# An encoder step on one core: the first weight unit ordered by hand, the seven-product scheme from the third group on, and a reciprocal root moved from GpSimd to VectorE

## The chip, the cores and the metric

The program runs on one core of a Trainium2 chip. The metric is the device time of one execution in microseconds; the time given is a median over runs, and the profile is of one further execution.

## The reference, cut to what matters

Two layers are applied to 512 prompt tokens and 64 sample tokens of width 1024, all in float32:

```python
# layer A (forgetting attention), layer B (gated MLP), each as x + mixer(rmsnorm(x)) @ w_out
z = h @ w_in_a            # q, k, v, gate (4 x 1024 columns) and 8 columns of forget logits
q, k = rmsnorm(q), rmsnorm(k)                     # per head of 128
logf = log_sigmoid(z[..., 4096:] + b_f)           # cumulated to a bias of the scores
o = softmax(q k^T * scale + f_q - f_k, causal) v  # sample rows also see 1024 cached keys
x = x + (o * silu(gate)) @ w_out_a

z = h @ w_in_b            # u, v, gate (3 x 2048 columns), v in 8 groups of 256 columns
v = rmsnorm(v)                                    # per group and row: needs 1/sqrt(mean square)
mixed = ws[g] (128 x 128, masked) applied to v over the rows of a chunk, + bs[g]
x = x + (u * mixed * silu(gate)) @ w_out_b
```

## The kernel before, in words

**Products.** Every float32 operand is split into a high part (rounded on ScalarE, `split`, L124) and a low part (the rest, on VectorE, L125). Each product is three TensorE matmuls: high by high, high by low, low by high. Weights come in units of 1 MB (two buffers `wraw`), and are split in pieces of 128x512 into `whi` and `wlo`; up to 8 pieces are held ahead (`PIECES`). Layer A has 20 units: four times k, q and v of two heads, four of the gate, four of the output. Layer B has 24 units (for each of 8 groups v, gate and u) and 8 of the output.

**Order.** Nothing is ordered by the program's text alone: when the kernel is built, a planner simulates the engines with its own costs and puts every instruction into its engine's queue at the moment when, in its simulation, it is ready; text order and a raised priority decide between ready ones. On the chip each queue then runs in exactly that order, and the head of a queue that waits holds up all behind it. Text order follows a clock of matmul time (`self.clock`): `later(delay, fn)` puts a step's text behind as much matmul work, with raised priority, except for the patient ones. `manual_schedule` makes the text order of an engine's instructions binding, and a manual dependency without a semaphore (`NOSYNC`) binds the order of two of them.

**First unit (k of heads 0 and 1).** The weights arrive in four DMAs, the tokens in tiles of 128 rows (the second tile's DMA between the second and third weight DMA, L208 to L211). A token tile is transposed in eight TensorE instructions (`turn_x`), scaled, and split. Tile 0 and the four weight pieces are ordered by hand in `run`; the turns of tiles 1 to 4 are called from `project_qk` through `next_x` with raised priority, and the planner places them. Squares of the tokens (`token_squares`, ScalarE, 1.06 us each) have no tie. The forget logits, carried in 16 extra columns, are finished in `forget`.

**MLP group (`group_in`).** `rows_product` makes v for four tiles of 128 rows (24 matmuls each) and the sample tile (16). The squares' sums go to `vz`; GpSimd scales them (L1175), VectorE makes the first guess of the root and GpSimd does three Newton rounds of four instructions (`rsqrt_pool`, L156 to L159). Then `split_scaled` makes `bvhi` (ScalarE) and `bvlo` (VectorE), and `mix` (raised priority, `MIX_DELAY` later) multiplies them by the group's 128x128 matrix into `s`, which VectorE takes to `mixed`. The gate unit is evicted through Silu into `gr`; GpSimd multiplies `gr` by `mixed` (L1215, 128x576, twice a group); the u unit is evicted by a product with `gr` into `pr` (L1201). Two of the four `mm` buffers in PSUM hold v until `split_scaled` has read it.

Gate and u of group 0 are plain: two halves of 128 columns by two halves of 288 tokens, 8 x 3 matmuls each, 96 in all (`cols_product`). From group `FAST_GROUP` = 1 on a seven-product scheme does it in 7 x 12 = 84 (`fast_product`), which needs sums of the weights (L236 to L241, VectorE) and of the tokens (`token_sums`: ten VectorE steps of 128x1152 in the still unused part of `pr`, L393, and four splits to `tparts`, in steps of `SUMS` = 2.4 us of the clock from group 0's gate on, as patient steps).

**Output of layer B (`out_b`).** It reuses the memory of the tokens and of `tparts` for the rows `xf`, the results `y` (3 buffers) and the split products `prhi`, `prlo`; a tile waits for what lay in its place.

Of the kernel before, what the change touches and what calls it, by code (L numbers as in the profile page):

```python
# [12 lines left out]
F32 = mybir.dt.float32  # L13
# [10 lines left out]
KT = 8  # L24
# [17 lines left out]
FORGET = (7.2, 11.7)  # L42
MIX_DELAY = 6.0
TURN = (5.3, 0.7)
# [4 lines left out]
PIECES = 8  # L49
FAST_GROUP = 1  # L50
SUMS = 2.4
# [8 lines left out]
class Program:  # L60
    def __init__(self, tc, io):
        self.tc = tc
        self.nc = tc.nc
        self.io = io
        self.clock = 0.0
        self.tasks = []
        self.count = 0
        self.count_y = 0
        self.patient = (self.sample_cache_values, self.gates_out, self.token_step)
# [52 lines left out]
    def split(self, hi, lo, src):  # L122

        self.nc.scalar.copy(hi, src)  # L124
        self.nc.vector.tensor_tensor(lo, src, hi.bitcast(F32), op=ALU.subtract)  # L125
# [7 lines left out]
    def rsqrt(self, z, pool, tag):  # L133

        v = self.nc.vector
        shape = list(z.shape)
        y = pool.tile(shape, F32, name=tag + "_y", tag=tag + "_y")
        t = pool.tile(shape, F32, name=tag + "_t", tag=tag + "_t")
        v.tensor_scalar(y.bitcast(I32), z.bitcast(I32), 1, None, op0=ALU.logical_shift_right)
        v.tensor_scalar(y.bitcast(I32), y.bitcast(I32), -1, MAGIC, op0=ALU.mult, op1=ALU.add)  # L140
        for _ in range(3):
            v.tensor_tensor(t, y, y, op=ALU.mult)
            v.scalar_tensor_tensor(t, in0=t, scalar=-0.5, in1=z, op0=ALU.mult, op1=ALU.mult)
            v.scalar_tensor_tensor(y, in0=t, scalar=1.5, in1=y, op0=ALU.add, op1=ALU.mult)
        return y

    def rsqrt_pool(self, z, pool, tag):

        v, p = self.nc.vector, self.nc.gpsimd
        shape = list(z.shape)  # L150
        y = pool.tile(shape, F32, name=tag + "_y", tag=tag + "_y")
        t = pool.tile(shape, F32, name=tag + "_t", tag=tag + "_t")
        v.tensor_scalar(y.bitcast(I32), z.bitcast(I32), 1, None, op0=ALU.logical_shift_right)
        v.tensor_scalar(y.bitcast(I32), y.bitcast(I32), -1, MAGIC, op0=ALU.mult, op1=ALU.add)
        for _ in range(3):
            p.tensor_tensor(t, y, y, op=ALU.mult)  # L156
            p.tensor_tensor(t, t, z, op=ALU.mult)  # L157
            p.tensor_scalar(t, t, -0.5, 1.5, op0=ALU.mult, op1=ALU.add)  # L158
            p.tensor_tensor(y, y, t, op=ALU.mult)  # L159
        return y  # L160
# [106 lines left out]
    def weights(self):  # L267

        self.held = 0
        self.fill()  # L270
# [16 lines left out]

    def rows_product(self, out, xhi, xlo, tile_no, w, extra=None):

# [5 lines left out]
        nkt = len(whi)  # L295
        for kt in range(nkt):
            s = slice(128 * tile_no, 128 * (tile_no + 1))
# [81 lines left out]
    def token_sums(self):  # L379
# [95 lines left out]
    def turn_x(self, pool, i):  # L475

        for half in range(2):
            self.turn_x_half(pool, i, half)

    def turn_x_half(self, pool, i, half):  # L480
# [51 lines left out]
    def forget(self, pool):  # L532
# [121 lines left out]
    def project_qk(self, p, is_q):  # L654
        nc, io, pool = self.nc, self.io, self.proj
        w = self.weights()
        name = "q" if is_q else "k"
# [29 lines left out]
        for grp in range(2):  # L687
            if first:
                src = pool.tile([128, 512], F32, name="nrm", tag="nrm", bufs=2)
                for i in range(2):  # L690
                    self.next_x()
                    ps = self.ps_mm()[:, :272]
                    self.rows_product(ps, *self.xparts, 2 * grp + i, w, self.whi0)
                    nc.scalar.copy(src[:, 256 * i:256 * (i + 1)], ps[:, :256])
                    self.forget_columns(2 * grp + i, ps)
            else:
                src = self.ps_mm()
                for i in range(2):
                    self.next_x()
                    self.rows_product(src[:, 256 * i:256 * (i + 1)], *self.xparts, 2 * grp + i, w)  # L700
# [4 lines left out]
        if first:  # L705
            self.rows_product(ps[:, :272], *self.xparts, 4, w, self.whi0)
            self.sample_rows(ps, pool, raw)
# [9 lines left out]
        for grp in range(3):  # L717
# [5 lines left out]
            for j in range(k):  # L723
                c = slice(128 * j, 128 * (j + 1))
                nc.vector.scalar_tensor_tensor(nrm[:, c], in0=srcs[grp][:, c], scalar=r[:n, 4 * grp + j:4 * grp + j + 1],
                                               in1=gain[:n], op0=ALU.mult, op1=ALU.mult)
            if not is_q and grp < 2:
# [11 lines left out]

    def next_x(self):  # L740
        if self.x_steps:
            self.x_steps.pop(0)()

# [368 lines left out]
    def group_in(self, g):  # L1112
# [49 lines left out]
        for grp in range(3):  # L1162
# [7 lines left out]
            else:  # L1170
# [25 lines left out]
        def gate(m, half, src):  # L1196
            nc.scalar.activation(grs[m][:, HALF * half:HALF * (half + 1)], src, AF.Silu)

        def product(m, half, src):
            out = self.pr[:, 2 * g + m, HALF * half:HALF * (half + 1)]  # L1200
            nc.vector.tensor_tensor(out, src, grs[m][:, HALF * half:HALF * (half + 1)], op=ALU.mult)  # L1201

# [26 lines left out]
    def out_b(self, pool):  # L1229
# [3 lines left out]
        for i in range(5):  # L1233
            n = 128 if i < 4 else NS
            xs.append(pool.tile([128, D], F32, name=f"xf{i}")[:n])
            nc.sync.dma_start(xs[i], self.x1d[i, :n, :])
        ys = pool.tile([128, 3, 512], F32, name="y")
        lows = pool.tile([NS, 512], F32, name="lows")

        parts = {}  # L1240
        for k in [14, 15, None] + list(range(14)):
            if k is None:
                pool.tile([128, 256], F32, name="unused")
                continue
            parts[k] = (pool.tile([128, NT + NS], F32R, name=f"prhi{k}"), pool.tile([128, NP], F32R, name=f"prlo{k}"))
# [9 lines left out]
        for j in range(2):  # L1255
            c = slice(512 * j, 512 * (j + 1))

            def finish(i, ps):
                y = ys[:xs[i].shape[0], self.count_y % 3, :]
                self.count_y += 1  # L1260
# [7 lines left out]
    def run(self):  # L1268
# [5 lines left out]
        with ExitStack() as top:  # L1274
# [47 lines left out]

            def step(i):
                with tc.high_priority(offset=XPRI):
                    self.turn_x(xp, i + 1)
                if i == 3:
                    for j in range(5):
                        self.token_squares(xp, j)
                    self.r_a, self.rb_a = self.token_scales(self.ss, "a")

            self.x_steps = [lambda i=i: step(i) for i in range(4)]
            self.project_qk(0, False)
# [81 lines left out]
```

## Time and profile before

| what | value |
|---|---|
| runs shown | median 823.99 us (822.27, 823.99, 825.94) |
| the profiled execution | 820.57 us |
| its span, first to last instruction | 818.6 us |
| TensorE busy | 786.3 us, 96% |
| VectorE, ScalarE, GpSimd busy | 67%, 46%, 24% |
| mean granted TensorE clock | 0.987 |

Times in the rows are microseconds from the span's start. A busy share says little of the kernel as a whole: TensorE is busy nearly always, so what can be saved there is idle time, time at the lower clock, or matmuls. In brackets behind an instruction stands how long its engine was idle before it and what ended the wait.

### The profile page before, as it was taken

The page shows a single profiled execution, that of the slowest core. Times are in us where ns is not written, and L with a number is a line of the kernel's source. Part 1 is how long each engine was busy: PE and PEld are TensorE (multiplying, and loading weights), DVE is VectorE, ACT ScalarE, POOL GpSimd, SP SyncE. Part 2 cuts the span into 40 slices and gives each one's busy share as a digit, 9 for nine tenths or more (in the row PEclk, how much of TensorE's full clock was granted, in tenths as well). Part 3 has the DMA queues.
Part 4 walks back from the last instruction along what each step waited for, and adds up shares of the span by engine and source line. Part 5 has one row for each costly group of instructions (what it writes and reads, how often), then busy time and mean ns, then how long its engine had stood idle before and what let it go on. Part 6 is the DMA issues. An engine that isn't in the chain of part 4 may idle for free.

```text
span 818.6 us, 14697 instructions
## 1 busy us (share of the span) xinstructions
PE 786.3 (96%) x5542; PEld 743.0 (91%) x5542; DVE 551.0 (67%) x1335; ACT 373.0 (46%) x875; POOL 195.4 (24%) x342
## 2 busy tenths in 40 slices
PE   6999999999999999998977999999999999899998
PEld 5999999999999998887967999999999999788886
DVE  4787767867675778449786677687778686862312
ACT  4545546464564557334441627363544445631210
POOL 1100723213235564000232323232232423100000
PEclk8999999999999999999989999999999999999999
DMA  8898653546434652644030233132333131533201
GB/s 214 110 111 146 179 90 85 116 95 61 100 67 144 205 169 80 216 149 170 7 116 8 67 100 113 56 110 65 103 104 111 56 106 55 187 136 117 95 1 58
DMA packets 73814, 87.60 MB, mean 107 GB/s; under 512 B 5224, under 2 KB 62336, under 8 KB 73744
## 3 DMA queue, kind: packets, MB, share of 16 engines
q1 hardware_dynamic: 73744, 86.67, 40.7%
q8 instruction: 43, 0.70, 0.3%
q14 instruction: 27, 0.22, 0.1%
HBM read 76.63 MB, written 10.03 MB: 106 GB/s over the span
## 4 chain that ended last, share of the span: by engine, by line
PE 85%; DVE 5%; POOL 3%; issue 2%; DMA 2%; ACT 2%; SPq 1%; POOLq 0%; DVEq 0%; ACTq 0%
PE mm L78 65%; PE s L78 13%; PE tr L82 4%; PE tr L78 2%; DMA wraw<-w_in_a 1%; DVE wlo L125 1%; DMA ts<-negs 1%; PE mm L82 1%; ACT whi L124 1%; POOL v_y L159 1%; POOL v_t L156 1%; DVE gt L982 1%; POOL v_t L157 1%; POOL v_t L158 0%; ACT sqv L1221 0%
## 5 line engine op out<-in xcount | busy, mean ns | idle before, releaser
L125 DVE TENSOR_TENSOR wlo<-wraw,whi 128x512 fp32r<-128x512 f32 x236 | 161.1, 702 | 91.1 <-ACT whi L124 87.5
L124 ACT CAST whi<-wraw 128x512 fp32r<-128x512 f32 x236 | 140.5, 620 | 158.3 <-PE mm L78 92.8
L78 PE MATMUL mm<-whi,xhi 128*128 128x256 f32 (+1 forms) x728 | 205.5, 287 | 4.1 <-DVE pr L1201 2.6
L78 PE MATMUL mm<-wlo,xhi 128*128 128x256 f32 x728 | 204.0, 285 | 0.0
L78 PE MATMUL mm<-whi,xlo 128*128 128x256 f32 (+1 forms) x640 | 183.2, 287 | 0.0
L78 PEld LDWEIGHTS mm<-whi,xhi 128*128 128x128 f32 x728 | 138.9, 191 | 5.4 <-DVE pr L1201 2.8
L78 PEld LDWEIGHTS mm<-wlo,xhi 128*128 128x128 f32 x728 | 138.7, 191 | 0.5
L78 PEld LDWEIGHTS mm<-whi,xlo 128*128 128x128 f32 x640 | 121.7, 190 | 0.6
L78 PE MATMUL mm<-xhi,whi 128*128 128x288 f32 x360 | 110.3, 307 | 0.8 <-DVE fq L371 0.8
L78 PE MATMUL mm<-xlo,whi 128*128 128x288 f32 x360 | 107.3, 298 | 0.0
L78 PE MATMUL mm<-xhi,wlo 128*128 128x288 f32 x360 | 107.2, 298 | 0.0
L78 PEld LDWEIGHTS mm<-xhi,whi 128*128 128x128 f32 x360 | 68.7, 191 | 1.4 <-DVE fq L371 1.1
L78 PEld LDWEIGHTS mm<-xlo,whi 128*128 128x128 f32 x360 | 68.8, 191 | 0.1
L78 PEld LDWEIGHTS mm<-xhi,wlo 128*128 128x128 f32 x360 | 68.6, 191 | 0.1
L770 POOL TENSOR_SCALAR tt<-nf,fq 128x128 f32<-128x128 f32 (+3 forms) x32 | 39.2, 1230 | 119.7 <-PE tr L82 66.6
L78 PE MATMUL mm<-thi,whi 128*128 128x288 f32 x224 | 67.0, 299 | 0.0
L78 PE MATMUL mm<-thi,wlo 128*128 128x288 f32 x224 | 66.3, 296 | 0.0
L78 PE MATMUL mm<-tlo,whi 128*128 128x288 f32 x224 | 66.2, 295 | 0.0
L1215 POOL TENSOR_TENSOR gr<-gr,mixed 128x576 f32<-128x576 f32 x16 | 27.4, 1720 | 93.4 <-DVE mixed L1156 93.1
L78 PE MATMUL mm<-whi,prhi 128*128 128x512 f32 x112 | 44.0, 393 | 1.8 <-ACT prhi L1251 1.2
L78 PE MATMUL mm<-wlo,prhi 128*128 128x512 f32 x112 | 43.8, 391 | 0.0
L78 PEld LDWEIGHTS mm<-tlo,whi 128*128 128x128 f32 x224 | 42.1, 188 | 0.0
(317 smaller groups left out, 1631.8 us busy)
## 6 DMA issues: line engine op xcount, KB each, us to landing
wraw<-w_in_b SPq DMA_DIRECT2D x24, 1024.0 KB, 5.2
wraw<-w_in_a SPq DMA_DIRECT2D x15, 1024.0 KB, 9.7
wraw<-w_out_b SPq DMA_DIRECT2D x8, 1024.0 KB, 5.2
kr<-cache_k SPq DMA_DIRECT2D x4, 1024.0 KB, 7.2
vr<-cache_v SPq DMA_DIRECT2D x4, 1024.0 KB, 5.3
wraw<-w_out_a SPq DMA_DIRECT2D x4, 1024.0 KB, 5.1
ts<-negs SPq DMA_DIRECT2D x8, 272.0 KB, 6.6
k_prompt<-nrm SPq DMA_DIRECT2D x8, 256.0 KB, 6.2
```

What stands on the lines that cost most here:

```text
L78: self.nc.tensor.matmul(out, lhs, rhs, start=start, stop=stop, skip_group_check=resumed)
L82: self.nc.tensor.transpose(out, src, self.ident[:n, :n])
L124: self.nc.scalar.copy(hi, src)
L125: self.nc.vector.tensor_tensor(lo, src, hi.bitcast(F32), op=ALU.subtract)
L156: p.tensor_tensor(t, y, y, op=ALU.mult)
L157: p.tensor_tensor(t, t, z, op=ALU.mult)
L159: p.tensor_tensor(y, y, t, op=ALU.mult)
L770: nc.gpsimd.tensor_scalar(t[:, :n], head["nf"][:, :n], self.fq[:, i, h:h + 1], None, op0=ALU.add)
L982: eng.tensor_tensor(g, g, self.ot[:, h, :], op=ALU.mult)
L1215: nc.gpsimd.tensor_tensor(grs[dt], grs[dt], mixed[dt], op=ALU.mult)
```

## The change

Constants: `MIX_DELAY` 6.0 to 3.0, `FAST_GROUP` 1 to 2. For v the GpSimd root is removed, and scaling and root run on VectorE. The first unit's TensorE order is written out (`first_rows`), its next unit's split is called behind the last token tile, with a tie; token squares are tied behind the casts of the next token tile; the forget chain behind the last norm of the first keys. The steps of the token sums are tied behind the latest eviction of a gate or u half, and use the `pr` rows of groups 4 to 7 as scratch (groups 2 to 5 before). `out_b` has four `y` buffers and no filler tile.

```diff
-MIX_DELAY = 6.0
+MIX_DELAY = 3.0
-FAST_GROUP = 1
+FAST_GROUP = 2
...
     def split_piece(self, n, i, src):
...
         self.split(hi, lo, src)
+        if n == 1:
+            self.tc.add_manual_dep(self.last_cast.ins, self.turned[4].ins.name, NOSYNC, reason="the tokens go first")
...
     def token_sums(self):
...
-        d3, d1, e3, e1 = (self.pr[:, 4 + 2 * n:6 + 2 * n, :].rearrange("p a (b t) -> p (a b) t", b=2) for n in range(4))
+        d3, d1, e3, e1 = (self.pr[:, 8 + 2 * n:10 + 2 * n, :].rearrange("p a (b t) -> p (a b) t", b=2) for n in range(4))
+        def behind(inst):
+
+            if self.last_taken is not None:
+                self.tc.add_manual_dep(inst.ins, self.last_taken.ins.name, NOSYNC, reason="spread out")
         def step(eng, out, a, b, op):
-            eng.tensor_tensor(out, a, b, op=op)
+            behind(eng.tensor_tensor(out, a, b, op=op))
         def done(n, src):
-            self.split(*self.tparts[n], src)
+            hi, lo = self.tparts[n]
+            behind(nc.scalar.copy(hi, src))
+            nc.vector.tensor_tensor(lo, src, hi.bitcast(F32), op=ALU.subtract)
...
     def token_squares(self, pool, i):
-        self.nc.scalar.activation(sq[:n], self.xin[i][:n], AF.Square, accum_out=self.ss[:n, i:i + 1])
+        square = self.nc.scalar.activation(sq[:n], self.xin[i][:n], AF.Square, accum_out=self.ss[:n, i:i + 1])
+        self.tc.add_manual_dep(square.ins, self.turned[min(i + 1, 4)].ins.name, NOSYNC, reason="the casts go first")
...
     def forget(self, pool):
-        nc.vector.tensor_tensor(f, self.fx, self.r_a.unsqueeze(2).broadcast_to(shape), op=ALU.mult)
+        first = nc.vector.tensor_tensor(f, self.fx, self.r_a.unsqueeze(2).broadcast_to(shape), op=ALU.mult)
+        self.tc.add_manual_dep(first.ins, self.last_norm.ins.name, NOSYNC, reason="the keys go first")
...
+    def first_rows(self, i, w):
+
+        a, b, c = range(0, 4), range(4, 6), range(6, 8)
+        order = {0: ((0, a), 1, (0, b), (1, a), (0, c)), 1: (2, (1, b), (1, c)), 2: ((2, a), 3, (2, b), (2, c)),
+                 3: ((3, a), 4, (3, b), (3, c))}[i]
+        with self.tc.manual_schedule(engines={mybir.EngineType.PE}):
+            for step in order:
+                if isinstance(step, int):
+                    self.turn_x(self.xpool, step)
+                else:
+                    n, kts = step
+                    if n not in self.first_sums:
+                        self.first_sums[n] = self.ps_mm()[:, :272]
+                    self.rows_product(self.first_sums[n], *self.xparts, n, w, self.whi0, kts)
+        if i == 3:
+            for j in range(5):
+                self.token_squares(self.xpool, j)
+            self.r_a, self.rb_a = self.token_scales(self.ss, "a")
+            self.fill()
+        return self.first_sums.pop(i)
...
     def group_in(self, g):
-        nc.gpsimd.tensor_scalar(z, z, 1.0 / 256, EPS, op0=ALU.mult, op1=ALU.add)
-        y = self.rsqrt_pool(z, small, "v")
+        nc.vector.tensor_scalar(z, z, 1.0 / 256, EPS, op0=ALU.mult, op1=ALU.add)
+        y = self.rsqrt(z, small, "v")
...
     def out_b(self, pool):
-        ys = pool.tile([128, 3, 512], F32, name="y")
+        ys = pool.tile([128, 4, 512], F32, name="y")
-        for k in [14, 15, None] + list(range(14)):
-            if k is None:
-                pool.tile([128, 256], F32, name="unused")
-                continue
+        for k in [14, 15] + list(range(14)):
```

## Rows read from the trace of the kernel before

**Rows 1.** Stretches: us; busy of PE, PEld, DVE, ACT, POOL; clock, DMA share, GB/s.
```profile
10.00:20.00 10.00, 6.36 (x33) 5.74 (x34) 6.49 (x13) 6.64 (x12) 0.00 (x0) 0.66 1.03 255
410.00:420.00 10.00, 8.78 (x67) 8.55 (x65) 9.20 (x14) 4.82 (x9) 2.78 (x6) 1.00 0.62 204
420.00:440.00 20.00, 13.53 (x75) 13.02 (x76) 14.26 (x28) 5.71 (x11) 5.41 (x18) 0.74 0.07 21
440.00:450.00 10.00, 7.41 (x62) 7.21 (x62) 5.71 (x8) 0.58 (x2) 2.77 (x2) 1.00 0.02 5
480.00:520.00 40.00, 40.00 (x318) 39.88 (x317) 30.91 (x62) 19.05 (x46) 10.52 (x23) 1.00 0.27 86
705.00:710.00 5.00, 3.49 (x26) 3.12 (x24) 3.91 (x11) 2.05 (x4) 1.55 (x2) 1.00 0.66 210
710.00:715.00 5.00, 3.61 (x13) 2.38 (x14) 5.00 (x10) 5.00 (x10) 1.71 (x1) 1.00 0.61 230
```

**Rows 2.** Timeline of TensorE, group 0: start, duration, instruction, idle before and releaser.
```profile
423.28 0.80 PE L78 MATMUL s<-wst,bvhi 128*128 128x256 f32 x2 [4.50 <-ACT bvhi L1225]
426.68 0.69 PE L78 MATMUL s<-wst,bvlo 128*128 128x128 f32 x2 [1.49 <-DVE bvlo L1226]
439.03 0.35 PE L78 MATMUL s<-whi,xhi 128*128 128x256 f32 x1 [1.70 <-DVE mixed L1156]
443.75 0.39 PE L78 MATMUL mm<-whi,xhi 128*128 128x256 f32 x1 [2.59 <-DVE pr L1201]
```

**Rows 3.** Chain that ended last, group 0: start, duration, what ran or was waited for.
```profile
406.90 8.47 PE mm L78 x64
...
415.56 1.81 DMA wsr<-ws
...
427.37 6.16 PE mm L78 x28
```

**Rows 4.** Timelines of GpSimd and VectorE in group 0, around the root and the gate product.
```profile
412.94 0.51 POOL L1175 TENSOR_SCALAR vz<-vz 128x5 f32<-128x5 f32 x1 [7.52 <-ACT sqv L1221]
...
414.58 1.35 DVE L393 TENSOR_TENSOR pr<-pr,xhi 128x1152 f32<-128x1152 f32 x1
...
439.29 3.48 POOL L1215 TENSOR_TENSOR gr<-gr,mixed 128x576 f32<-128x576 f32 x2
439.60 1.92 DVE L238 TENSOR_TENSOR wraw<-wraw 128x512 f32<-128x512 f32 x1
```

**Rows 5.** Timelines of GpSimd and TensorE in group 5.
```profile
610.52 0.54 POOL L1175 TENSOR_SCALAR vz<-vz 128x5 f32<-128x5 f32 x1 [9.51 <-ACT sqv L1221]
...
616.44 0.20 POOL L159 TENSOR_TENSOR v_y<-v_y,v_t 128x5 f32<-128x5 f32 x1
...
617.20 0.50 PE L78 MATMUL s<-wst,bvhi 128*128 128x256 f32 x2 [0.17 <-ACT bvhi L1225]
```

**Rows 6.** Timeline of VectorE: first and last of eleven root instructions, twice.
```profile
54.65 0.17 DVE L139 TENSOR_SCALAR h_y<-hz 128x10 int32<-128x10 int32 x1
...
57.59 0.17 DVE L144 SCALAR_TENSOR_TENSOR h_y<-h_t,h_y 128x10 f32<-128x10 f32 x1
...
87.08 0.17 DVE L139 TENSOR_SCALAR h_y<-hz 128x10 int32<-128x10 int32 x1
...
92.11 0.16 DVE L144 SCALAR_TENSOR_TENSOR h_y<-h_t,h_y 128x10 f32<-128x10 f32 x1
```

**Rows 7.** Timelines of TensorE and ScalarE, first unit.
```profile
16.45 1.09 PE L82 MATMUL tr<-ident,xt 128*128 128x128 f32 x4 [2.10 <-DVE wlo L125]
...
11.46 1.06 ACT L506 ACTIVATE xsq<-xt 128x1024 f32<-128x1024 f32 x1 [2.46 <-DMA xt<-x_prompt]
...
14.47 0.62 ACT L124 CAST whi<-wraw 128x512 fp32r<-128x512 f32 x1 [0.31 <-DMA wraw<-w_in_a]
...
24.36 1.14 ACT L124 CAST whi<-wraw 128x512 fp32r<-128x512 f32 x2 [0.60 <-DMA wraw<-w_in_a]
```

**Rows 8.** Timeline of GpSimd, end of group 7.
```profile
708.45 3.26 POOL L1215 TENSOR_TENSOR gr<-gr,mixed 128x576 f32<-128x576 f32 x2 [14.02 <-DVE mixed L1156]
```

More of the change, by code (lines that the diff above doesn't have):

```diff
@@ L67, in __init__ @@
         self.count = 0
+        self.last_taken = None
         self.count_y = 0
@@ L122, in split @@
     def split(self, hi, lo, src):
-        self.nc.scalar.copy(hi, src)
+        self.last_cast = self.nc.scalar.copy(hi, src)
         self.nc.vector.tensor_tensor(lo, src, hi.bitcast(F32), op=ALU.subtract)
@@ L144, in rsqrt @@
             v.scalar_tensor_tensor(y, in0=t, scalar=1.5, in1=y, op0=ALU.add, op1=ALU.mult)
[L145 to L159, printed above, removed]
         return y
@@ L264, in split_piece, with weights @@
         self.split(hi, lo, src)
+        if n == 1:
+            self.tc.add_manual_dep(self.last_cast.ins, self.turned[4].ins.name, NOSYNC, reason="the tokens go first")
         self.queue.append(([hi[:, q, :] for q in range(k)], [lo[:, q, :] for q in range(k)]))
-    def weights(self):
+    def weights(self, fill=True):
         self.held = 0
-        self.fill()
+        if fill:
+            self.fill()
         his, los = [], []
@@ L284, in block, with rows_product @@
         return self.queue.pop(0)
-    def rows_product(self, out, xhi, xlo, tile_no, w, extra=None):
+    def rows_product(self, out, xhi, xlo, tile_no, w, extra=None, kts=range(KT)):
         whi, wlo = w
@@ L295, in rows_product @@
         nkt = len(whi)
-        for kt in range(nkt):
+        for kt in kts:
             s = slice(128 * tile_no, 128 * (tile_no + 1))
@@ L478, in turn_x @@
             self.turn_x_half(pool, i, half)
+        self.turned[i] = self.last_cast
     def turn_x_half(self, pool, i, half):
@@ L655, in project_qk @@
         nc, io, pool = self.nc, self.io, self.proj
-        w = self.weights()
+        w = self.weights(p or is_q)
         name = "q" if is_q else "k"
@@ L690, in project_qk @@
                 for i in range(2):
-                    self.next_x()
-                    ps = self.ps_mm()[:, :272]
-                    self.rows_product(ps, *self.xparts, 2 * grp + i, w, self.whi0)
+                    ps = self.first_rows(2 * grp + i, w)
                     nc.scalar.copy(src[:, 256 * i:256 * (i + 1)], ps[:, :256])
@@ L698, in project_qk @@
                 for i in range(2):
-                    self.next_x()
                     self.rows_product(src[:, 256 * i:256 * (i + 1)], *self.xparts, 2 * grp + i, w)
@@ L705, in project_qk @@
         if first:
-            self.rows_product(ps[:, :272], *self.xparts, 4, w, self.whi0)
+            with self.tc.manual_schedule(engines={mybir.EngineType.PE}):
+                self.rows_product(ps[:, :272], *self.xparts, 4, w, self.whi0)
             self.sample_rows(ps, pool, raw)
@@ L724, in project_qk @@
                 c = slice(128 * j, 128 * (j + 1))
-                nc.vector.scalar_tensor_tensor(nrm[:, c], in0=srcs[grp][:, c], scalar=r[:n, 4 * grp + j:4 * grp + j + 1],
-                                               in1=gain[:n], op0=ALU.mult, op1=ALU.mult)
+                self.last_norm = nc.vector.scalar_tensor_tensor(
+                    nrm[:, c], in0=srcs[grp][:, c], scalar=r[:n, 4 * grp + j:4 * grp + j + 1], in1=gain[:n],
+                    op0=ALU.mult, op1=ALU.mult)
             if not is_q and grp < 2:
@@ L738, in forget_columns @@
         self.nc.vector.tensor_reduce(self.fx[:n, i, :], cols, axis=AX.X, op=ALU.add)
-    def next_x(self):
-        if self.x_steps:
-            self.x_steps.pop(0)()
+    def first_rows(self, i, w):
+        a, b, c = range(0, 4), range(4, 6), range(6, 8)
+        order = {0: ((0, a), 1, (0, b), (1, a), (0, c)), 1: (2, (1, b), (1, c)), 2: ((2, a), 3, (2, b), (2, c)),
+                 3: ((3, a), 4, (3, b), (3, c))}[i]
+        with self.tc.manual_schedule(engines={mybir.EngineType.PE}):
+            for step in order:
[10 more added lines that the diff above has]
+            self.r_a, self.rb_a = self.token_scales(self.ss, "a")
+            self.fill()
+        return self.first_sums.pop(i)
     def begin_attention(self, p):
@@ L1196, in gate @@
         def gate(m, half, src):
-            nc.scalar.activation(grs[m][:, HALF * half:HALF * (half + 1)], src, AF.Silu)
+            self.last_taken = nc.scalar.activation(grs[m][:, HALF * half:HALF * (half + 1)], src, AF.Silu)
         def product(m, half, src):
             out = self.pr[:, 2 * g + m, HALF * half:HALF * (half + 1)]
-            nc.vector.tensor_tensor(out, src, grs[m][:, HALF * half:HALF * (half + 1)], op=ALU.mult)
+            self.last_taken = nc.vector.tensor_tensor(out, src, grs[m][:, HALF * half:HALF * (half + 1)], op=ALU.mult)
         def form(take):
@@ L1258, in finish @@
             def finish(i, ps):
-                y = ys[:xs[i].shape[0], self.count_y % 3, :]
+                y = ys[:xs[i].shape[0], self.count_y % 4, :]
                 self.count_y += 1
@@ L1321, in run @@
                 self.warm_up(scratch, WARM[1])
[L1323 to L1331, printed above, removed]
+            self.xpool, self.first_sums, self.turned = xp, {}, {}
             self.project_qk(0, False)
```

## The prediction, made before the changed kernel ran

> **What bounds the kernel now.** I first read the table of stretches. From 480 to 520 us TensorE is busy 40.00 of 40 us and takes 318 instructions, 0.126 us each, while VectorE is busy 31 us and ScalarE 19 [rows 1]: in the MLP groups the matmul stream is the limit, and a faster GpSimd, VectorE or ScalarE is worth nothing there unless TensorE waits for it. So I looked for stretches in which TensorE is not full. There are three, and the change touches all of them: 10 to 20 us (33 instructions in 10 us, granted clock 0.66), 420 to 440 us (75 instructions in 20 us, clock 0.74), and 705 to 715 us (7.10 busy of 10 us) [rows 1].
>
> Then the timeline of TensorE for the worst, group 0 of the MLP: four waits, 4.50, 1.49, 1.70 and 2.59 us, the first two for `bvhi` and `bvlo`, the scaled v, the third for `mixed`, the last for a product taken out of PSUM [rows 2]. The chain that ended last says what lies behind the first: not a matmul but the DMA of `wsr`, 1.81 us [rows 3]. GpSimd's queue shows why. It scaled `vz` at 412.94, after waiting 7.52 us for the squares [rows 4]; the Newton rounds of the root stood behind a clearing of the next group's `wsr`, whose data had yet to land. VectorE was crowded as well: a token sum of 1.35 us started at 414.58, between the two instructions of the first guess [rows 4]. TensorE got its `bvhi` at 423.28, 10.3 us after `vz`.
>
> **The first MLP group (root on VectorE, sums tied, `MIX_DELAY`).** What is lost: the first wait of 4.50 us began at 418.78, so 1.2 us of it lie before 420. From 420 to 440 there are 75 instructions, which at 0.126 us take 9.4 us, so 10.6 us are lost [rows 1]; behind 440 the last wait adds 2.6 [rows 2]. Together 14.4 us. About 10.3 of these are the four waits, the rest is the clock: 28 matmuls of 288 columns took 6.16 us (0.220 each) behind the wait, 64 of them 8.47 us (0.132 each) ahead of it [rows 3].
>
> With the change the root has no GpSimd instruction, so the wait for `wsr` is no longer in the chain. The eleven VectorE root instructions exist in the trace on 128x10: 3.1 us from first to last in one place, 5.2 us in another, amid other VectorE work [rows 6]. The token sums (fourteen steps, ten of 1.35 us) go behind evictions of halves, one per 24 matmuls of 0.132 us, so at most two or three fall into the root instead of a stretch that is busy 9.20 of 10 us [rows 1]. Scale, root and two scaling steps then end some 6 us after the squares instead of 10.3, and the squares themselves start earlier, because the row sums before them no longer queue behind sums of tokens. TensorE meanwhile has the rest of the gate half to do, and the planner's placing of `mix` was only 4.5 us too early. If the scaled v comes in time, `mixed` and the gate product follow at once, and the third and fourth wait go too. What is late next is VectorE itself: the remaining sums must be done before group 2's gate, a whole group later (of 299 instructions in the seven-product form, 112 for v, 168 for gate and u, 18 for `mix`, 1 turn, 37.7 us at 0.126, and 24 matmuls more in the plain form), so they have room. I take 12.9 us, leaving 1.5 us (one sum of 1.35 us in the wrong place). Bounds: 0 (the planner again places `mix` too early) and 14.4.
>
> What it costs: group 1 is plain, 2 x 12 = 24 matmuls of 288 columns more, at 0.132 us [rows 3]: +3.2 us. It is on the path, as TensorE is full there. Against it stand six casts and six low parts fewer and eight sums of weights fewer in that group; they lie beside matmuls, and I cost them at nothing.
>
> **The later groups.** In group 5 `vz` starts at 610.52 and GpSimd's last root instruction at 616.44, and TensorE waited 0.17 us for `bvhi` [rows 5]. The planner's place for `mix` thus fits the chain almost exactly. On VectorE the chain is 1 to 3 us shorter by the two examples [rows 6], the planner sees that too, and TensorE stays full: 0 us. Eight groups get 12 small instructions each, about 0.2 us apart, some 2.4 us of a group's 37.7; VectorE has a quarter of its time free [rows 1], and nobody waits for it. If that cover is gone, it costs up to the rival below.
>
> A rule of the Trainium skill bears on this. The trace first: while GpSimd ran the two gate products (3.48 us from 439.29), a VectorE sum of 128x512 took 1.92 us, more than a token sum of 128x1152 (1.35) [rows 4]. The Trainium skill, "SBUF — State Buffer", in its section on the two sides of SBUF, says that VectorE and GpSimd share a port pair under an exclusive lock: a VectorE instruction with two SBUF inputs and a GpSimd one that reads SBUF exclude each other for a whole instruction. By that rule the root moved to VectorE, three of whose steps square a tile in SBUF, could be held by a gate product, one product at most (about 1.7 us). In group 7 the products start at 708.45 [rows 8], far from any root, so I add nothing; the rule only makes the rival below a little likelier.
>
> **The first unit.** From 10 to 20 us 33 instructions make 4.2 us of full-rate work; the second token tile is there only at 11.5, so at most 10 - 4.2 - 1.5 = 4.3 us can come back [rows 1]. Two reasons are visible. ScalarE stood 2.46 us before a token square at 11.46 with casts queued behind it, and TensorE stood 2.10 us at 16.45 before the turn of the third token tile, with products of tile 0 behind it in the queue [rows 7]. The ties put the squares behind the casts, and the hand order puts 24 products of tile 0 and 12 of tile 1 ahead of that turn. The limit that stays is the fourth weight piece, cast at 14.47 when it landed [rows 7]. I estimate 3 us from this. Against it: the next unit's weights landed and were cast at 24.36, ahead of the last token tile [rows 7]; now these casts follow the last tile's, which I put at about 27 us, and the squares may come ahead of them. TensorE reaches them at about 30, so I charge 1 us. Net -2.0 us; bounds -4.3 and +2.5 (all four casts late at 0.6 us each). The forget chain moves behind the keys' norms, some 6 us later; it lies beside the q products, where TensorE is full, and I cost it at nothing.
>
> **The end.** In group 7 the gate products start at 708.45 after waiting 14.02 us for `mixed` [rows 8], and TensorE idles 2.9 us between 705 and 715 [rows 1]. An earlier `mix` brings that forward by what the root saves, 1 to 3 us: I take -1.5, bounds 0 and -2.9. The new layout in `out_b` shifts each split product by 1 KB, so that it overlaps two of the token sums' tiles; they are read for the last time at least 24 matmuls before the end of group 7, which hides it, except for the last one.
>
> **The sum.** -12.9 + 3.2 - 2.0 - 1.5 = -13.2 us. The profiled execution took 820.57 us (span 818.6 and 2 us around it), so it would take 807.4; the median of the runs is 3.4 us above that execution, so 811 us is forecast. With all bounds at the good end (-14.4, -4.3, -2.9) it is -18.4, or 806.
>
> **Rivals.**
>
> *Half of it stays.* TensorE's place for `mix` is the planner's, and it was 4.5 us wrong in group 0. With the tied sums still falling into VectorE's queue, the wait could shrink only to half. For: VectorE is the busiest helper there [rows 1]. Against: the `wsr` wait, the part the planner missed most, is gone. -7.0 + 3.2 - 1.0 - 0.7 = -5.5: 818.5 us.
>
> *The change does not do what it says.* The wait in group 0 stays whole, because something else is as late as the root was; only 24 matmuls, the first unit and the end count: +3.2 - 2.0 - 1.5 = -0.3: 823.7 us.
>
> *The first unit drops to the lower clock.* The hand order has small waits at each weight piece. In 10 to 20 us the granted clock was 0.66, so a part ran at the lower of the two levels, 1.2 GHz, after waits of about 2 us [rows 1, 7]. With 60 matmuls more at 0.22 instead of 0.126 us (5.6 us), the first unit costs about +4 instead of -2: 817 us. Against: the waits of 1.70 and 2.59 us at 439 and 444 us [rows 2] left the clock at 1.00 from 440 to 450 [rows 1]. The Trainium skill, "TensorE: Matmul & The Clock Gate" (section on PSUM-queue depth-cycling), tells of a kernel whose clock swung between its two levels because TensorE idled briefly and often between groups of matmuls. By that rule the first unit would be slowed as in this rival; the waits just named do not bear it out.
>
> *Slower.* `MIX_DELAY` lets `mix` stand 3 us earlier in TensorE's queue, in every group, and in group 5 it had 0.17 us to spare the wrong way [rows 5]. If the real VectorE chain, in a queue that is three quarters full, is no shorter than GpSimd's was (5.2 us is close to the 5.9 between 610.52 and 616.44 [rows 5, 6]) and the planner thinks it is, TensorE waits up to 3 us in each of the seven later groups: +21 us, 832 us. It makes the kernel slower by over 0.5% from (13.2 + 4.1) / 7 = 2.5 us a group on. Against: in group 5 `mix` began 6.7 us behind the scaling of `vz`, which itself waits for the last rows of v, so it stood more than 6 us behind v: the planner goes by readiness, and the delay is only a floor.
>
> **How the numbers follow.** Forecast 0.60 (alone 804 to 816), half 0.14, first unit 0.07, no change 0.08, slower 0.11. What a measurement can tell from no change is about 0.5%, 4.1 us: forecast, half and first unit are faster, 0.81; same 0.08; slower 0.11. The range 804 to 822 takes in the first three.
>
> **What would show it.** Right: no wait for `bvhi` in group 0 and clock 1.00 from 410 to 450; more than 60 instructions of TensorE from 10 to 20 us; 24 matmuls more; a group still takes 38 us from group 2 on. Wrong: waits before `mix` in every group, or a wait for `whi` near 30 us, or VectorE's sums late for group 2.

## The result, and the profile after

The changed kernel takes 815.88 us (median; 813.93 to 817.89) against 824.59 us beside it: ratio 0.9897, interval 0.9859 to 0.9936, so 8.7 us or 1.0% faster. The forecast was 811 us, the range 804 to 822; the time lies at the edge of the band of the forecast alone (804 to 816). The profiled execution took 817.46 us (820.57 before), with a span of 815.7 us and a mean granted clock of 0.985. TensorE has 5566 matmuls in it, 24 more than before, GpSimd 157 us of work instead of 195.

The sum hides two opposite movements. I used two instructions that stand in both traces as markers: A, the turn of layer B's tokens that waits for `xlo`, and B, a matmul of group 7 that waits for VectorE's sum `fq`. They are lines of TensorE's timeline; first the kernel before, then the one after:

```profile
380.68 0.66 PE L82 MATMUL tr<-ident,h 128*128 128x128 f32 x4 [1.86 <-DVE xlo L125]
...
707.18 0.40 PE L78 MATMUL mm<-xhi,whi 128*128 128x288 f32 x1 [0.53 <-DVE fq L371]
```

```profile
387.19 1.12 PE L83 MATMUL tr<-ident,h 128*128 128x128 f32 x4 [1.86 <-DVE xlo L126]
...
704.21 0.40 PE L79 MATMUL mm<-xhi,whi 128*128 128x288 f32 x1 [0.57 <-DVE fq L360]
```

From A to B 326.5 us have become 317.0: 9.5 us gained, though 24 matmuls at 0.132 us (3.2 us) were added, so 12.7 without these. But A itself is reached 6.5 us later, where the first unit was to bring it 2 us forward.

**Where the loss is.** The table of stretches of the kernel after (columns as in [rows 1]) shows the first unit better than before, 50 instructions from 10 to 20 us instead of 33, and then a hole. From 60 to 70 us there are 35 instructions at a clock of 0.66; the kernel before had 88 there at 1.00. 53 instructions of 0.126 us are 6.7 us.

```profile
10.00:20.00 10.00, 8.85 (x50) 8.16 (x49) 6.85 (x12) 5.65 (x10) 0.00 (x0) 0.66 1.06 259
...
40.00:50.00 10.00, 10.00 (x85) 9.77 (x84) 7.78 (x29) 2.52 (x5) 0.11 (x1) 1.00 0.99 111
50.00:60.00 10.00, 9.24 (x75) 8.48 (x73) 5.71 (x25) 4.74 (x12) 0.11 (x1) 1.00 0.93 114
60.00:70.00 10.00, 6.27 (x35) 6.05 (x36) 7.19 (x19) 3.22 (x6) 0.00 (x0) 0.66 0.91 100
...
410.00:420.00 10.00, 10.00 (x80) 10.00 (x79) 9.33 (x17) 7.01 (x14) 1.91 (x3) 1.00 0.36 119
420.00:440.00 20.00, 18.17 (x134) 18.06 (x133) 14.53 (x35) 5.55 (x13) 5.85 (x11) 0.93 0.33 90
440.00:450.00 10.00, 10.00 (x84) 10.00 (x84) 8.51 (x10) 4.08 (x9) 0.00 (x0) 0.98 0.17 58
```

The chain that ended last names the cause, a store:

```profile
43.61 1.08 DVE nrm L722 x5
44.69 17.73 DMA k_prompt<-nrm
...
62.55 1.14 DVE nrm L722 x4
63.69 0.04 issue
63.73 5.44 PE mm L79 x26
```

The first keys' norms are written to two tiles `nrm` (two buffers) and stored from there. The norms of the first q want the same two buffers, so VectorE waited for the store to end, and TensorE for VectorE, 4.49 us:

```profile
63.73 0.58 PE L79 MATMUL mm<-whi,xhi 128*128 128x256 f32 x1 [4.49 <-DVE nrm L722]
...
436.50 0.36 PE L79 MATMUL s<-whi,xhi 128*128 128x256 f32 x1 [1.83 <-DVE mixed L1171]
```

The buffers were shared before too, but there the eight stores of `k_prompt` took at most 9.5 us to land, and the first was down at 57.5 us, 1.8 us before q's norm at 59.29. The queue of transfers shows what else moved, before and after:

```profile
28.45 0.38 SPq L208 DMA_DIRECT2D wraw<-w_in_a  x1
...
41.20 0.37 SPq L208 DMA_DIRECT2D wraw<-w_in_a  x1
...
48.88 1.80 SPq L728 DMA_DIRECT2D k_prompt<-nrm  x2
```

```profile
32.79 0.38 SPq L194 DMA_DIRECT2D wraw<-w_in_a  x1
...
37.85 0.37 SPq L194 DMA_DIRECT2D wraw<-w_in_a  x1
...
44.69 3.04 SPq L726 DMA_DIRECT2D k_prompt<-nrm  x2
```

The tie of the second unit's casts puts its low parts from 25.27 to 30.27 us, its `wraw` buffer is free later, and the next load is issued 4.3 us later. The load behind that one is issued 3.4 us earlier and the store 4.2 us earlier, and neither gains by it. How long the second load took from issue to landing stands in the view of the tile `wraw`, for this one load, before and after:

```profile
DMA to landing us min/median/max: 15.3/15.3/15.3
```

```profile
DMA to landing us min/median/max: 23.5/23.5/23.5
```

The two loads of 1 MB land one behind the other, some 14 us apart, at 42.7 and 56.5 us before and at 47.4 and 61.3 after; the first store lands 1.1 us behind the second of them, at 57.5 and 62.4. In e2 and e4 below it lands 0.7 us behind it. So the store's 17.7 us instead of 8.6 are 4.2 us of earlier issue and 4.9 us by which the loads ahead of it in the queue came in later. This is read from the landing times; no run moves those loads alone. The DMA engines are 93 to 99% busy from 40 to 60 us, at 111 to 114 GB/s, but they were 90 to 100% busy before as well, at 87 to 137.

**Where the gain is.** In group 0 there are 298 instructions from 410 to 450 us, where 204 stood [rows 1]. Of four waits [rows 2] one is left, 1.83 us for `mixed` (at 436.50, shown above). The token sums are what moved on VectorE. Before, seven of their 14 steps started between 411 and 431 us, around root and `bvlo`; the first, the last and one between from VectorE's timeline:

```profile
411.42 1.36 DVE L125 TENSOR_TENSOR tlo<-pr,thi 128x1152 fp32r<-128x1152 f32 x1 [0.18 <-ACT thi L124]
...
424.87 1.36 DVE L393 TENSOR_TENSOR pr<-pr,xhi 128x1152 f32<-128x1152 f32 x1
...
429.77 1.34 DVE L125 TENSOR_TENSOR tlo<-pr,thi 128x1152 fp32r<-128x1152 f32 x1
```

After, three stand between 415 and 422 us, and then none until `mixed` is made. The last before this gap and the first behind it:

```profile
420.32 1.35 DVE L387 TENSOR_TENSOR pr<-pr,xhi 128x1152 f32<-128x1152 f32 x1
...
438.38 2.18 DVE L387 TENSOR_TENSOR pr<-pr 128x1152 f32<-128x1152 f32 x1
```

Half of the sums now run from 438 to 453 us, behind everything that TensorE waited for.

### The profile page after: what moved, and what is told of

The parts are those of the page before. It is cut to its first block, busy times and chain, and to the rows that moved or that the text cites. A ratio compares the mean times of both kernels' runs of the same rounds, so it can differ in the third digit from the quotient of the medians.

```text
span 815.7 us, 14678 instructions
## 1 busy us (share of the span) xinstructions
PE 789.3 (97%) x5566; PEld 747.0 (92%) x5566; DVE 551.8 (68%) x1395; ACT 370.6 (45%) x863; POOL 156.9 (19%) x238
## 4 chain that ended last, share of the span: by engine, by line
PE 87%; DVE 5%; DMA 5%; issue 1%; ACT 1%; POOL 1%; SPq 1%; POOLq 0%; DVEq 0%; ACTq 0%
PE mm L79 67%; PE s L79 14%; PE tr L83 4%; DMA k_prompt<-nrm 2%; PE tr L79 2%; DMA ts<-negs 1%; PE mm L83 1%; DVE wlo L126 1%; DMA wraw<-w_in_a 1%; DVE gt L997 1%; DVE pr L1216 0%; DVE fsum L590 0%; DVE nrm L722 0%; DMA negs<-fsum 0%; POOL cv L925 0%
## 5 line engine op out<-in xcount | busy, mean ns | idle before, releaser
L79 PE MATMUL mm<-xhi,whi 128*128 128x288 f32 x400 | 120.8, 302 | 0.6 <-DVE fq L360 0.6
L79 PE MATMUL mm<-xlo,whi 128*128 128x288 f32 x400 | 118.0, 295 | 0.0
L79 PE MATMUL mm<-xhi,wlo 128*128 128x288 f32 x400 | 117.8, 295 | 0.0
L79 PEld LDWEIGHTS mm<-xhi,whi 128*128 128x128 f32 x400 | 75.1, 188 | 1.0 <-DVE fq L360 0.7
L79 PEld LDWEIGHTS mm<-xlo,whi 128*128 128x128 f32 x400 | 75.3, 188 | 0.0
L79 PEld LDWEIGHTS mm<-xhi,wlo 128*128 128x128 f32 x400 | 75.0, 188 | 0.1
L79 PE MATMUL mm<-thi,whi 128*128 128x288 f32 x192 | 57.1, 298 | 0.0
L79 PE MATMUL mm<-tlo,whi 128*128 128x288 f32 x192 | 56.7, 295 | 0.0
L79 PE MATMUL mm<-thi,wlo 128*128 128x288 f32 x192 | 56.4, 295 | 0.0
L79 PE MATMUL mm<-whi,prlo 128*128 128x512 f32 x96 | 36.6, 392 | 0.6 <-DVE prlo L1264 0.6
```

The source lines that it names most:

```text
L79: self.nc.tensor.matmul(out, lhs, rhs, start=start, stop=stop, skip_group_check=resumed)
```

## The experiments

Two questions were tested: what made the loss (theory: the shared buffer; rival: the hand order as such), and what made the gain (my reason was the root leaving GpSimd; rivals: the ties, the plain second group). Times are medians; the ratio to the kernel before, with its interval, stands behind. The last two columns are the time to A and from A to B, read from each profile. From A to B the profiles fall in two classes: 326 us without the ties, 313 to 318 with them. Within a class little can be told from one profile: the change, e1, e3 and e8 have the same layer B and read 317.0, 314.9, 316.1 and 313.3.

| kernel | us | ratio | to A | A to B |
|---|---|---|---|---|
| before, beside the changed kernel | 824.59 | | 380.7 | 326.5 |
| the change | 815.88 | 0.9897 (0.9859 to 0.9936) | 387.2 | 317.0 |
| e1 own tiles for the first keys | 809.85 | 0.9835 (0.9803 to 0.9866) | 380.5 | 314.9 |
| e2 first unit alone | 824.23 | 1.0016 (0.9993 to 1.0038) | 381.9 | 326.0 |
| e3 MLP part alone | 813.43 | 0.9882 (0.9850 to 0.9914) | 382.0 | 316.1 |
| e4 root back on GpSimd | 815.24 | 0.9900 (0.9868 to 0.9932) | 385.6 | 317.4 |
| e5 e1, seven products from group 1 | 809.87 | 0.9844 (0.9799 to 0.9889) | 381.5 | 314.8 |
| e6 e1, sums untied | 819.28 | 0.9954 (0.9928 to 0.9979) | 382.3 | 326.2 |
| e7 e1, `MIX_DELAY` 6 | 810.12 | 0.9840 (0.9796 to 0.9885) | 381.3 | 314.9 |
| e8 e1, forget chain untied | 809.48 | 0.9841 (0.9802 to 0.9880) | 383.3 | 313.3 |
| e9 e1, own tile for the sample keys too | 819.33 | 0.9946 (0.9928 to 0.9964) | 394.2 | 316.0 |
| e10 the ties of the sums alone | 816.30 | 0.9917 (0.9902 to 0.9933) | 385.8 | 318.4 |
| e11 e9, next unit's casts untied | 821.02 | 0.9967 (0.9945 to 0.9988) | 393.2 | 317.2 |
| e12 e9, seven products from group 1 | 819.65 | 0.9957 (0.9933 to 0.9981) | 390.4 | 315.6 |

**e1, own tiles for the first keys.** Only the place of the two tiles changes:

```diff
-                src = pool.tile([128, 512], F32, name="nrm", tag="nrm", bufs=2)
+                src = self.xpool.tile([128, 512], F32, name=f"knrm{grp}")
```

> The changed kernel with one edit: the two tiles that hold the first keys get a place of their own in the memory of the tokens, so that the norms of the first q need not wait until the keys' store has read them. If the loss in the first 80 us is that wait (4.5 us idle and some 2 to 3 us at the lower clock behind it), the wait of TensorE near 64 us goes and the span falls from 815.7 by 6 to 7 us, to about 809. If the transfers themselves are what is late (the weights in the same queue), the wait moves to a weight piece and the span stays at 814 or more.

The wait at 63.73 us is gone and A comes at 380.5 us, 6.7 us earlier, with TensorE's order nearly the same. The store itself is as slow as ever, 16.6 to 17.0 us to landing, but nobody waits for it. So the buffer was the cause, not the hand order. A smaller wait of the same kind takes its place, for the sample rows' store (chain of waits, then TensorE's timeline):

```profile
48.05 14.56 DMA k_sample<-nrms
...
62.89 0.34 DVE nrms L722
63.23 1.14 DVE fp L571
```

```profile
64.42 0.41 PE L83 MATMUL tr<-ident,fp 8*128 8x8 f32 x4 [2.13 <-DVE fp L571]
```

**e2 and e3, the two parts alone.** e2 is the kernel before with the first unit's part only (`first_rows`, its ties, the forget chain's tie); e3 has everything else (constants, root, ties of the sums, `out_b`). Their edits are the two halves of the diff of the change, and are not printed again.

> The kernel before with only the first unit's part of the change (hand order, ties of squares, of the next unit's casts and of the forget chain). If that part loses by itself, TensorE is ahead by 1.5 to 2 us at 40 us, waits for the first q's norms near 60 us, and the span is 5 to 7 us over the 818.6 of before (about 825). If the wait came only by the planner's luck in the whole change, the span is 816 to 819.

> The kernel before with only the later parts: root on VectorE, MIX_DELAY 3, plain group 1, tied sums, the output's buffers. If the two parts of the change simply add, this is the changed kernel without the loss in the first unit: 9 to 10 us under before (span about 809, ratio 0.988). If they depend on each other, it is within 4 us of before.

e2 met the same store (16.0 us to landing) and waited 2.73 us at 61.95, not 4.49, and its clock stayed at 1.00 from 60 to 70 us. It lost 0.6 us instead of the 5 to 7 I expected: its layer A is that of the change, so the size of the loss differs by execution, with how late the store lands and with the clock behind the wait. e3 came as expected. The parts add up to -10.2 + 0.6 = -9.6 us; the whole measured -8.7. The first unit's part, as it was made, is worth nothing. With the tiles apart it is worth something: e1 is 3.6 us under e3 by the medians, though their intervals overlap.

**e4, root back on GpSimd.** The changed kernel with the old root for v, otherwise the same:

```diff
-        nc.vector.tensor_scalar(z, z, 1.0 / 256, EPS, op0=ALU.mult, op1=ALU.add)
-        y = self.rsqrt(z, small, "v")
+        nc.gpsimd.tensor_scalar(z, z, 1.0 / 256, EPS, op0=ALU.mult, op1=ALU.add)
+        y = self.rsqrt_pool(z, small, "v")
```

> The changed kernel with scaling and root of v on GpSimd again, the rest as changed. If the gain of group 0 comes from taking the root out of GpSimd's queue, where it stood behind the clearing of the next matrix, TensorE again waits for the scaled v in group 0 and the span is 5 to 12 us over 815.7. If it comes from the plain second group and the tied sums, which leave VectorE and ScalarE free, the span stays within 2 us of 815.7.

815.24 us, and no wait for `bvhi` at all. GpSimd's timeline, group 0:

```profile
408.06 0.15 POOL L1134 MEMSET wsr<- 64x64 f32 x1 [0.16 <-DMA wsr<-ws]
...
413.15 0.89 POOL L1205 TENSOR_SCALAR vz<-vz 128x5 f32<-128x5 f32 x1 [3.72 <-ACT sqv L1251]
...
421.49 0.20 POOL L165 TENSOR_TENSOR v_y<-v_y,v_t 128x5 f32<-128x5 f32 x1
```

Its root took 8.5 us and was in time all the same. My reason for the gain falls, but for one part: the planner had put the clearing that waits for `wsr` elsewhere in this queue, so that wait did not recur. e10 has it again.

**e6, e10, the ties.** e6 is e1 with the tie of the sums off; e10 is the kernel before with nothing but that tie (and the scratch rows that it needs):

```diff
-            if self.last_taken is not None:
+            if False:
```

> e1 without the ties of the token sums (they run as early as the planner finds room), second group plain. If the ties emptied group 0 of waits, TensorE waits again for the scaled v there, 4 us or more, and the span is 811 to 818. If the plain second group did it, the span stays within 2 us of 806.8.

> The kernel before with only the ties of the token sums (and their scratch rows); root on GpSimd, MIX_DELAY 6, second group in the seven-product form. If the ties are what emptied group 0, the waits for the scaled v (4.50 and 1.49 us) and most of the slow clock go, the wait for a product (2.6 us) stays: span 808 to 811. If the ties need the root on VectorE or the plain group, it is 814 or more.

e6 loses 9.4 us against e1, somewhat more than expected (its span is 819.9 us), and the old waits are back, although the root is on VectorE. TensorE's timeline of e6:

```profile
426.75 0.80 PE L79 MATMUL s<-wst,bvhi 128*128 128x256 f32 x2 [5.52 <-ACT bvhi L1240]
428.17 0.69 PE L79 MATMUL s<-wst,bvlo 128*128 128x128 f32 x2 [0.62 <-DVE bvlo L1241]
...
441.81 0.35 PE L79 MATMUL s<-whi,xhi 128*128 128x256 f32 x1 [1.60 <-DVE mixed L1171]
```

and VectorE's, in which token sums of 1.36 us stand between the root's steps of 0.17 us:

```profile
420.69 0.17 DVE L144 SCALAR_TENSOR_TENSOR v_t<-v_t,vz 128x5 f32<-128x5 f32 x1
421.00 1.36 DVE L392 TENSOR_TENSOR tlo<-pr,thi 128x1152 fp32r<-128x1152 f32 x1
422.27 0.16 DVE L145 SCALAR_TENSOR_TENSOR v_y<-v_t,v_y 128x5 f32<-128x5 f32 x1
422.39 1.36 DVE L387 TENSOR_TENSOR pr<-pr,xhi 128x1152 f32<-128x1152 f32 x1
423.67 0.16 DVE L143 TENSOR_TENSOR v_t<-v_y 128x5 f32<-128x5 f32 x1
423.78 1.36 DVE L387 TENSOR_TENSOR pr<-pr,xlo 128x1152 f32<-128x1152 f32 x1
425.06 0.16 DVE L144 SCALAR_TENSOR_TENSOR v_t<-v_t,vz 128x5 f32<-128x5 f32 x1
```

e10 gains 8.1 us from A to B with root, `MIX_DELAY` and `FAST_GROUP` as before; its waits in group 0 are 0.36, 0.15, 0.52, 1.83 and 1.51 us. The tie alone does nearly all. It also tries what e4 left open: the clearing stands between scaling and root again and waits for `wsr`, and TensorE's wait for `bvhi` is 0.36 us all the same. GpSimd's timeline, before and in e10:

```profile
417.48 0.14 POOL L1104 MEMSET wsr<- 64x64 f32 x1 [4.03 <-DMA wsr<-ws]
```

```profile
414.61 1.16 POOL L1183 TENSOR_SCALAR vz<-vz 128x5 f32<-128x5 f32 x1 [6.03 <-ACT sqv L1229]
...
418.37 0.34 POOL L1112 MEMSET wsr<- 64x64 f32 x2 [2.60 <-DMA wsr<-ws]
```

What the ties bring forward most is the start: `vz` is scaled 32.3 us behind A before and 34.1 in e6, but 27.5 to 29.2 us behind it in e4, e10 and the change. From there to the end of the root it takes 9.8 us before, 9.1 in e6, 9.0 in e10, 8.5 in e4 and 7.1 in the change.

The profile of e10 is 5 us longer than I expected, for a reason far from the change. Up to 92 us TensorE runs as in the kernel before, within 0.1 us; then it waits 3.20 us at 100.02 us for `ptlo` of the first attention, and the clock is 0.50 from 100 to 105. GpSimd comes late there, as it scales the tile `ts` 3.5 us later than before (before, then e10):

```profile
90.47 3.05 POOL L836 TENSOR_SCALAR ts<-ts,fqs 128x1088 f32<-128x1088 f32 x1 [3.77 <-ACT pthi L124]
```

```profile
94.00 3.05 POOL L844 TENSOR_SCALAR ts<-ts,fqs 128x1088 f32<-128x1088 f32 x1 [7.17 <-DMA wraw<-w_in_a]
```

The loads of `ts` are issued 2.7 us later (81.89 for 79.23) and land at 93.7 instead of 90.2. They stand in the queue behind a transfer that waits for the small store of `negs`, and that store took 4.7 us to land here, at most 2.5 in the kernel before. Why it did is not shown; the queues hold the same order up to there. By the medians nothing is lost: e10 is 7.4 us under the kernel before beside it (816.30 and 823.66), whose 23 executions lie between 818.9 and 828.6, so the profile of before is one of the faster.

**e5 and e12, the seven products from group 1 again.**

```diff
-FAST_GROUP = 2
+FAST_GROUP = 1
```

> e1 (own place for the first keys' rows) with FAST_GROUP 1: the second group takes the seven-product form again, sums stay tied. If the plain second group is what emptied group 0 of waits, the waits of before come back (4 to 10 us in 415 to 450 us, some by late sums of tokens or weights), less 3.2 us of matmuls saved: span 808 to 814. If the ties alone did it, the 24 matmuls are saved and the span is 806.8 - 3.2 = 803.6.

> e9 with FAST_GROUP 1. As in e5 against e1, the 3.2 us of saved matmuls should be given back by the wait for a product at the start of the second group (2.6 us): within 1.5 us of e9. If it is 2 us or more below e9, the plain second group costs net.

e5 equals e1 (809.87 and 809.85), and neither of the two cases expected came whole. It saves the 24 matmuls (3.2 us) and gives them back in waits of 0.40 and 2.56 us, the latter with VectorE the late one:

```profile
435.18 0.39 PE L79 MATMUL mm<-whi,xhi 128*128 128x256 f32 x1 [2.56 <-DVE pr L1216]
```

e12 says the same of e9. With the ties on, the plain second group is neither a gain nor a loss.

**e7 and e8, two constants of the order.** `MIX_DELAY` back to 6.0, and the forget chain without its tie:

```diff
-MIX_DELAY = 3.0
+MIX_DELAY = 6.0
...
-        self.tc.add_manual_dep(first.ins, self.last_norm.ins.name, NOSYNC, reason="the keys go first")
```

> e1 with MIX_DELAY 6 as before. If the planner places the mixing products by readiness and the delay is only a floor, the span stays within 2 us of 806.8. If the shorter delay is what moved them, waits before the mixing products or at the end of group 7 change, by 3 us or more.

> e1 without the tie of the forget chain behind the first keys. In e1 TensorE waits 2.13 us at 64.4 us for the scan of the forget values. If the tie made them late, that wait shrinks or goes and the span falls by 1 to 2 us, to about 805.5. If VectorE's queue there is the limit whatever its order, it stays at 806.8.

Both equal e1 within 0.4 us. The delay is only a floor, as the prediction had it; the tie of the forget chain is not what makes `fp` late (that wait is 2.37 us without it).

**e9 and e11, the rest of the store's neighbourhood.** e9 also moves the sample keys' norms to a tile of their own; e11 is e9 without the tie of the next unit's casts:

```diff
-                n, k, nrm = NS, 2, pool.tile([NS, 256], F32, name="nrms", tag="low")
+                n, k = NS, 2
+                nrm = (self.xpool.tile([NS, 256], F32, name="knrms") if first else
+                       pool.tile([NS, 256], F32, name="nrms", tag="low"))
...
-        if n == 1:
-            self.tc.add_manual_dep(self.last_cast.ins, self.turned[4].ins.name, NOSYNC, reason="the tokens go first")
```

> e1 with a place of its own for the first keys' sample rows as well (their store took 14.6 us to land in e1, and the scan of the forget values stood behind the norm that waited for that buffer). If the remaining wait of 2.13 us at 64.4 us is the same mechanism, it goes and the span is about 804.5. If the scan is late by itself, the wait stays and the span is 806 to 808.

> e9 without the tie of the second unit's casts behind the last token tile. If that tie delays the raw buffer's release and so the third and fourth weight loads, these start some 4 us earlier, and if they matter the span falls by 1 to 2 us below e9; if they are covered it stays within 1.5 us; if the casts now hold up the tokens, it rises by 1 to 3 us.

e9 missed. Its wait for `fp` shrinks to 1.35 us, but the planner now issues the load of `past` at 53.35 us, behind a weight load, where e1 issued it ahead of that, at 51.14; TensorE waits for it:

```profile
71.70 1.01 PE L83 MATMUL tr<-ident,past 128*8 128x128 f32 x4 [7.38 <-DMA past<-cache_logf]
```

A tile that only moves a buffer moved the planner's order and cost 9.5 us. e11 came as its third case: 1.7 us over e9 by the medians, though the intervals overlap, with 6.03 us lost in the first unit at 27.80, waiting for `xhi`. With the hand order the casts need their tie. It does show that the tie is what moves the load: without it the load is issued at 28.22 us, with it (e9) at 32.85. What the later load does to the store it does not show, as the loads behind it moved too.

## Why the prediction was right, and where not

**The total** fell in the range, 4.9 us above the forecast. By the medians of the two halves, the later parts gave -10.2 us (e3) where -12.9 + 3.2 - 1.5 = -11.2 was forecast, and the first unit +0.6 (e2) where -2.0 was: most of what is missing is the first unit's. The two profiles say where. The same number of TensorE instructions had begun 1.8 us earlier at 59 us; the wait for the store and the slow clock behind it cost 6.8, the wait for `ptlo` at 102.90 us 1.0, the way from there to A 0.5, so A is 6.5 late; A to B gives -9.5 and the end 0. That makes -3.0 for this pair of executions (span 818.6 to 815.7); by the medians it is -8.7, since the profiled execution of before was 3.4 us under its median and this one 1.6 over.

Of the signs named, no wait for `bvhi` in group 0, 24 matmuls more and groups of 38 us came. More than 60 instructions from 10 to 20 us did not (50), nor the clock of 1.00 from 410 to 450 us (0.93 from 420 to 440).

**The first MLP group: the size about right, the first reason wrong.** -12.9 + 3.2 was forecast, and A to B measured -12.7 + 3.2. That they agree so closely is luck: other profiles with the same layer B give up to 3.7 us more, and 1.3 us of it belongs to the later groups. The step "the wait for `wsr` is no longer in the chain" is not what gave it: with the root on GpSimd (e4, e10) the gain is there, in e10 with that wait, and with the root on VectorE and no tie (e6) it is not. What does it is the step I put second, the sums behind evictions, with what I said of the squares, that they start earlier. I had named one sum of 1.35 us [rows 4]; seven of the 14 stood in those 20 us, 9.5 us of VectorE's time.

**The later groups** were forecast at 0. From the first use of `bvhi` in group 2 to that in group 7, TensorE takes 189.9 to 190.4 us in the four kernels with the root on GpSimd (before, e2, e4, e10) and 188.3 to 188.5 in all ten with it on VectorE, e7 with its `MIX_DELAY` of 6 among them. So the root's move is worth 1.3 to 1.9 us, some 0.3 a group. Only waits of 0.17 us for `bvhi` in some groups show part of it [rows 5]; the rest is not traced.

**"On VectorE the chain is 1 to 3 us shorter" failed in the later groups.** In group 0 it holds by a little (7.1 us against 8.5 in e4). In group 7 it took 6.7 us (684.32 to 690.99), against 6.1 in [rows 5]: the steps are 0.17 us each, but splits of 0.7 us stand between them. It cost nothing, because the planner put `mix` behind 96 matmuls of the gate instead of 72. With the chain no shorter, the term of -1.5 us at the end came to 0: the gate product of group 7 comes 3.0 us earlier, as B does, and not more.

**The plain second group** costs the 3.2 us, but I set the relief of VectorE against it at nothing; e5 shows that the relief is worth about the same 3.2 us.

**The first unit** gained 2.3 to 2.5 us at 17 to 25 us and 1.7 to 2.1 at 28 to 59, by the time at which the same number of TensorE instructions had begun; -2.0 was forecast. The charge for the late casts was the mis-sized term: I priced 1 us for TensorE's wait for `whi` and not the buffer that these casts free, and the next load behind it. Nor did I follow the moved norms to their stores and ask who wants their tiles next. It cost about 7 us at 60 to 70 us. That the shared tile makes the wait is shown by e1; that the tie moves the load, by e11; that the later load makes the store land late is read from the landing times only. The further wait of 1.88 us at 102.90, for `ptlo`, is not the first unit's: e3, whose first unit is that of before, has 1.64 us there.

**The rivals.** No step of group 7's root took more than 0.17 us, so no gate product held it; GpSimd ran nothing from 674 to 691 us, so the rule that I had drawn on had nothing to act on there. A sum was slow: the one at 438.38 took 2.18 us instead of 1.35, beside the gate product of 2.79 us that GpSimd began at 436.56. That agrees with the rule of the Trainium skill, "SBUF — State Buffer" (the section on the two sides of SBUF), that a VectorE instruction with two SBUF inputs and a GpSimd one that reads SBUF exclude each other; nobody waited for that sum. The lower clock of the third rival did come, not in the first unit but behind the wait for the store (0.50 from 62 to 68 us). "Slower" did not: no wait for `bvhi` stands in group 0, and e7 shows the delay to be idle.

**The best kernel** is e1 (e5, e7 and e8 equal it): 809.85 us, 13.7 us or 1.65% under the kernel before.

## What to carry to other kernels

Small work that is only loosely due belongs behind a tie where it can't fall into a short chain that the bounding engine waits for; where the chain runs mattered less here (some 0.3 us a group). When a step is moved, follow its buffers as well as its result: which tile it frees, which load waits for that, which store stands behind that load, and who writes next to the tile that a store still reads. An order written by a planner can shift when a single tile gets another place, so take a gain of a few us as real only after looking for the waits that came and went elsewhere.

## What was not expected of the hardware

A store of two halves of 256 KB took 16 to 18 us to land behind weight loads (e1, e2, the change), and 8.6 us in the kernel before, where the loads ahead of it landed 4.9 us earlier. Once the load ahead had landed (92.0 us in e1), a store of the same size, issued at 92.60 us, took 2.1. The stretch around it has the DMA engines 90 to 100% busy at 84 to 137 GB/s; from 10 to 20 us they moved 255 GB/s [rows 1].

The clock fell after some waits and not after others of the same length. The wait of 1.83 us for `mixed` is in the change and in e1. In the change the clock was 0.50 from 438 to 440 us:

```profile
436.00:438.00 2.00, 1.50 (x9) 1.54 (x10) 0.54 (x3) 0.00 (x0) 1.54 (x3) 0.77 0.30 44
438.00:440.00 2.00, 2.00 (x12) 2.00 (x11) 1.99 (x2) 0.14 (x1) 1.35 (x1) 0.50 0.95 232
440.00:442.00 2.00, 2.00 (x17) 2.00 (x17) 2.00 (x3) 1.52 (x3) 0.00 (x0) 0.88 0.72 246
```

and in e1, with its wait at 428.84, it was 1.00 throughout:

```profile
420.00:440.00 20.00, 18.15 (x148) 17.83 (x147) 15.58 (x27) 6.38 (x12) 3.81 (x6) 1.00 0.21 63
```

So the waits of 1.70 and 2.59 us that left the clock alone [rows 1, 2] were a weak argument against the third rival.
